# Feeding the first up block of a ConvFFN with the unnormalised residual

## The chip, the cores and the metric

The kernel runs on one core of a Trainium2 chip. Its time is the device time of one execution in microseconds; the number given for a kernel is the median of its runs. The engines are TensorE (PE in the profile, its weight loads PEld), VectorE (DVE), ScalarE (ACT), GpSimd (POOL) and SyncE (SP, which issues the loads of the weights). All of them run their own instructions in a fixed order and wait for each other by semaphores.

## The reference

The layer works on 256 latent tokens (with 256 context tokens beside them) of width 2048, in fp32. Only its second half matters here:

```
x = x + mod_x[2] * merge_branches(...)                     # gated residual; ends in @ w_out
x = x + mod_x[5] * conv_ffn(modulate(x, g_ffn, mod_x[3], mod_x[4]), w_up, conv_w, conv_b, w_down)

mod_x = split(silu(c) @ w_mod + b_mod, 6)                  # shift, scale, gate; twice
modulate(x, g, shift, scale) = rms_norm(x, g) * (1 + scale) + shift
conv_ffn(h): u = h @ w_up                                  # 2048 -> 2 x 5632
             u = depthwise conv of width 3 over the tokens, + conv_b
             a, g = split(u, 2);  return (silu(a) * g) @ w_down
```

The normalisation divides each token by the root of its mean square. So modulate(x) = r(token) * [x * g * (1 + scale)] + shift, and h @ w_up = r(token) * ([x * g * (1 + scale)] @ w_up) + shift @ w_up.

## The kernel before

Every product is fp32 taken apart into two fp32r halves, high and low, and summed from three products: high by high, low by high and high by low. Weights come from memory in pieces of 256 rows by 512 columns (512 KB, `wload`, issued by SP into seven buffers called raw). `wsplit` makes the halves of a piece: ScalarE copies the high part (L61, tile whi), VectorE subtracts to get the low part (L62, tile wlo), into three buffers each. One such piece for one projection is a tick: eight ticks make a block of 512 columns over all 2048 rows.

`tick` is where other work is put between the products. `defer(n, fn)` runs fn at the (n+1)th tick from now; matrix products and transposes issued there (`mm_b`, `turn_b`) are pinned behind the last product of the tick before. `bg_steps` is a list of small steps of which a tick takes `bg_rate` on average. The order on each engine is made by a planner that takes the ready instruction of highest priority by its own estimate of times; priority is program order, and the splitting of weights is raised above everything else.

The modulation vectors of the latent tokens are made by such steps (`mod_latent`): a step loads two raw pieces ahead, and VectorE multiplies the two 512-wide rows of one piece by a column of silu(c) and adds them up (L305 and L307, tile macc); after eight steps the sum is turned and reduced (L311, L313), and a deferred part sums it over partitions with a small product (tile pcl) and writes four columns. Three of the vectors (shift2, scale2, gcol1) are made during the mixing stages at a rate of 0.3, then 0.52, in the order 3, 4, 2; the fourth (gcol2, the last gate) at 0.36 in the up stage, 32 steps.

The output projection (`w_out`, four blocks, `proj_nat`) evacuates each bank by VectorE: times the gate (L920), added to the residual x1 (L921), and ScalarE sums the squares (L922). One and two ticks later TensorE turns the 128 x 512 result (`turn`, L81, tile ptx) and ScalarE copies it to x1T (L929). The gate as rows is made at the fifth tick of the first of these blocks (`rows_from_cols`, two small DMAs of GpSimd's queue).

Behind the four blocks the kernel finishes what is deferred (`flush`, L936), sums the squares (L938), makes the token factor (`rms_scale`, L353 to L359), spreads it over the partitions by a product with a diagonal (`token_rows`, L367 to L370, tile pr) and makes the input h2: for each of the 16 row tiles, VectorE scales (L417), ScalarE adds the shift and rounds to the high half (L418), VectorE makes the low half (L419). Then the up projection follows (`proj_pair`): 11 blocks, each of a side 0 (the half that goes through silu) and a side 1 (the other half). A tick here has 16 products of 128 x 512 or 256. `up_evac` adds the two halves of a bank (L973, L974), does the convolution (L975, L976, L978), and silu (L983) or the product of the sides (L985) and the split of the result. Six blocks make the first half and are followed by their part of the down projection; then come five blocks and the rest.

PSUM has eight banks: four of tag acc, one of tag main and three of tag side. In the up stage side 0 takes the four acc banks, side 1 takes main and the three side banks (tile accs). The deferred sums of gcol2 use main and are let in on side 0 only. The large SBUF tiles come from one pool of 16 (`M`).

Of the kernel before, what the change touches and what calls it, by code (L numbers as in the profile page):

```python
# [30 lines left out]
def layer_kernel(ctx, tc, A, out):  # L31
# [108 lines left out]

    beside = []
    later = []

    def defer(n, fn):

# [6 lines left out]
    def tick():  # L152

        pin[0] = last[0]
        for e in later:
            e[0] -= 1
        due = [e for e in later if e[0] < 0]
        later[:] = [e for e in later if e[0] >= 0]
        for e in due:
            e[1]()  # L160
        if beside:
            beside[2] += beside[1]
            while beside[2] >= 1.0:
                beside[2] -= 1.0
                next(beside[0], None)
        bg_rate[1] += bg_rate[0]
        while bg_rate[1] >= 1.0 and bg_steps:
            bg_rate[1] -= 1.0
            bg_steps.pop(0)()
        pin[0] = None  # L170
# [109 lines left out]

        return [lambda k0=k0: step(k0) for k0 in range(0, KT, nk)]

    def mod_latent(parts, put=lambda fn: defer(3, fn)):


        seq = [(part, dst, j, k0) for part, dst in parts for j in range(4) for k0 in range(0, KT, 2)]
        raws, a = {}, []

        def get(i):
            if i < len(seq) and i not in raws:  # L290
                part, _, j, k0 = seq[i]
                c0 = part * D + j * 512
                raws[i] = wload(w_mod[k0 * P:k0 * P + 256, c0:c0 + 512])

        def step(i):
            part, dst, j, k0 = seq[i]
            get(i)
            get(i + 1)
            if k0 == 0:
                a[:] = [W2("mod", "macc", [P, 512])]  # L300
            raw = raws[i]
            for k in range(2):
                kt = k0 + k
                if kt == 0:
                    V.tensor_scalar(a[0], raw[:, 0, :], ccol[:, 0:1], None, op0=ALU.mult)  # L305
                else:
                    V.scalar_tensor_tensor(a[0], raw[:, k, :], ccol[:, kt:kt + 1], a[0],  # L307
                                           op0=ALU.mult, op1=ALU.add)
            if k0 == KT - 2:
                tr = W2("mod", "mtr", [P, 16, 32])  # L310
                V.transpose(tr.rearrange("p a c -> p (a c)"), a[0])  # L311
                rs = sm.tile([P, 16], F32, name="mrs", tag="mrs", bufs=2)
                V.tensor_reduce(rs, tr, op=ALU.add, axis=AX.X)  # L313

                def out():
                    pc = bank("pcl", (32, 16))
                    mm_b(pc, sel[:, 0:32], rs, start=True, stop=True)
                    pv = pc.rearrange("p (a b) -> p b a", b=4)
                    d = dst[:, 4 * j:4 * j + 4]
                    for b4 in range(4):  # L320
                        V.tensor_copy(d[32 * b4:32 * b4 + 32, :], pv[:, b4, :])
                    b0 = part * 16 + j * 4
                    V.tensor_tensor(d, d, bmod[:, b0:b0 + 4], op=ALU.add)

                put(out)

        return [lambda i=i: step(i) for i in range(len(seq))]
# [16 lines left out]
    scale2 = cst.tile([P, KT], F32, name="scale2")  # L344
    gcol1 = cst.tile([P, KT], F32, name="gcol1")
    gcol2 = cst.tile([P, KT], F32, name="gcol2")

    def rms_scale(ss, n, shape):

# [321 lines left out]
        return vh, vl  # L671


    bg_steps.extend(mod_latent(((3, shift2), (4, scale2), (2, gcol1))))
    bg_rate[:] = [0.3, 0.0]

    qbt = M("qb", [P, 8, T])
# [203 lines left out]
    for j in range(4):  # L881
# [27 lines left out]
    x1 = [M(f"x1_{t}", [P, D]) for t in range(2)]  # L909
    for t in range(2):  # L910
        nc.sync.dma_start(x1[t], A["x"][0][t * P:(t + 1) * P, :])
    gate1 = []
    defer(4, lambda: gate1.append(rows_from_cols("gate1", gcol1)))
    x1T = [M(f"x1T{i}", [P, 8, T]) for i in range(2)]
    ss1 = sm.tile([P, 2, 4], F32, name="ss1", bufs=1)
    for j in range(4):
        def wo_evac(t, b, j=j):
            js = slice(j * 512, (j + 1) * 512)
# [5 lines left out]
            def turn():  # L924
                pt = bank("ptx1", (P, 4, P), side=True)
                for k in range(4):
                    turn_b(pt[:, k, :], x1[t][:, j * 512 + k * P:j * 512 + (k + 1) * P], ident)
                dst = x1T[j // 2][:, (j % 2) * 4:(j % 2) * 4 + 4, t * P:(t + 1) * P]
                S.activation(dst, pt, AF.Copy)  # L929
# [8 lines left out]
    V.tensor_reduce(s1, ss1, op=ALU.add, axis=AX.X)  # L938
# [20 lines left out]
    w_up, w_down = A["w_up"][0], A["w_down"][0]  # L959
    for half, blocks in enumerate((range(0, 6), range(6, 11))):  # L960
        n = len(blocks)
        ah = [M("ah", [P, 8, T], F32R) for _ in range((n + 1) // 2)]
        al = [M("al", [P, 8, T], F32R) for _ in range((n + 1) // 2)]
        for i, j in enumerate(blocks):
            u = [[W2("fc", "u", [P, 2, T]) for _ in range(2)] for _ in range(2)]

            def up_evac(f, b, side, j=j, u=u, i=i, ah=ah, al=al):
# [4 lines left out]
                us = W2("fa", "us", [P, T])  # L972
                S.activation(us, b[:, T:2 * T], AF.Copy)  # L973
                V.tensor_tensor(us, b[:, 0:T], us, op=ALU.add)  # L974
                S.activation(d, us, AF.Identity, scale=cw1[:, fi:fi + 1], bias=cb[:, fi:fi + 1])  # L975
                V.scalar_tensor_tensor(d[:, 1:T], us[:, 0:T - 1], cw0[:, fi:fi + 1], d[:, 1:T],  # L976
                                       op0=ALU.mult, op1=ALU.add)
# [9 lines left out]
                    split(ah[i // 2][:, q, :], al[i // 2][:, q, :], uu)  # L987

            for side in range(2):
                proj_pair(w_up, side * DFF + j * 512, ALL, lambda kt: h2[kt // 4][:, kt % 4, :, :],  # L990
                          up_banks(side), lambda f, b, side=side: up_evac(f, b, side))
        if half == 0:
            assert not bg_steps
            while sums:
                sums.pop(0)()
            flush()
            gate2 = rows_from_cols("gate2", gcol2)
        for j in range(4):
# [64 lines left out]
```

## Time and profile before

| what | value |
|---|---|
| median of 3 runs | 2040.28 us (2038.79 to 2041.38) |
| span of the profiled execution, first to last instruction | 2036.9 us |
| difference of the two | 3.4 us |
| TensorE busy | 1978.8 us, 97% |
| VectorE busy | 1429.5 us, 70% |
| ScalarE busy | 961.1 us, 47% |
| granted TensorE clock, mean | 0.993 |
| read from memory | 409.63 MB |

The page names its profiled execution by its span alone; the 3.4 us lie around it. Times in rows are counted from the start of the span. In a row of the timeline stand start, duration, engine, line, operation, result and inputs, count, and in brackets how long the engine had been idle and what released it. TensorE's matmuls overlap, so a group of four ends later than the sum of what each costs. A row of a view by stage gives the start and end, the length, and the busy time of each engine in that stretch.

### The profile page before, as it was taken

What the parts mean: (1) busy time and instruction counts of PE and PEld (TensorE: products, weight loads), DVE (VectorE), ACT (ScalarE), POOL (GpSimd) and SP (SyncE); (2) the same over time, 40 slices, a digit from 0 to 9 for tenths busy, and PEclk for the clock granted to TensorE, in tenths of its full rate; (3) what the DMA queues carried; (4) which work ended last, traced back from release to release, by engine and by line L of the source; (5) the groups of instructions that cost most, each with busy time, mean ns of one, the idle gap of its engine ahead of it and who ended that gap; (6) DMA issues with size and microseconds to landing.
All of it is one profiled execution on the core that took longest, in us unless ns stands there. A gap on an engine that the chain in (4) does not pass through costs nothing.

```text
span 2036.9 us, 27383 instructions
## 1 busy us (share of the span) xinstructions
PE 1978.8 (97%) x10384; PEld 1644.1 (81%) x10384; DVE 1429.5 (70%) x2237; ACT 961.1 (47%) x1394; POOL 42.5 (2%) x62
## 2 busy tenths in 40 slices
PE   6999999999999999999999999899999999999998
PEld 4678888887787777887787878688888888888887
DVE  4657577877748888877776455888887555667754
ACT  3323464553345556444344444565555434556532
POOL 0001000101000000000000000000000000000000
PEclk8999999999999999999999999899999999999999
DMA  9977223236544456788886655577775656555563
GB/s 351 355 259 232 86 83 93 87 121 207 182 137 133 125 171 217 249 281 275 273 276 227 236 199 188 193 249 247 265 254 196 212 193 194 187 187 187 194 211 111
DMA packets 214340, 413.54 MB, mean 203 GB/s; under 512 B 12548, under 2 KB 21092, under 8 KB 213184
## 3 DMA queue, kind: packets, MB, share of 16 engines
q1 hardware_dynamic: 212320, 406.89, 60.5%
q0 software_dynamic: 1360, 4.74, 0.8%
q8 instruction: 81, 1.33, 0.3%
q14 instruction: 51, 0.42, 0.1%
q10 hardware_dynamic: 528, 0.17, 0.0%
HBM read 409.63 MB, written 2.11 MB: 202 GB/s over the span
## 4 chain that ended last, share of the span: by engine, by line
PE 56%; DMA 8%; DVE 5%; issue 1%; ACT 0%; DVEq 0%; ACTq 0%
PE acc L68 40%; PE accs L68 12%; DMA raw<-in_w_mod 8%; DVE macc L307 2%; DVE wlo L62 1%; PE poa L78 1%; PE pS L78 1%; PE ptp L81 1%; PE pto L81 0%; ACT whi L61 0%; PE ptq L81 0%; DMA raw<-in_w_gla_o 0%; PE ptx L81 0%; DVE macc L305 0%; DVE s L811 0%
## 5 line engine op out<-in xcount | busy, mean ns | idle before, releaser
L61 ACT ACTIVATE whi<-raw 128x1024 fp32r<-128x1024 f32 x568 | 601.1, 1059 | 792.7 <-PE acc L68 623.5
L62 DVE TENSOR_TENSOR wlo<-raw,whi 128x1024 fp32r<-128x1024 f32 x568 | 693.0, 1224 | 324.5 <-ACT whi L61 303.4
L307 DVE SCALAR_TENSOR_TENSOR macc<-raw,ccol,macc 128x512 f32<-128x512 f32 x240 | 180.5, 752 | 116.1 <-DMA raw<-in_w_mod 112.3
L68 PE MATMUL acc<-h,whi 128*128 128x512 f32 x704 | 178.3, 395 | 2.2 <-DVE h L419 2.2
L68 PE MATMUL accs<-h,whi 128*128 128x512 f32 x704 | 176.3, 392 | 0.0
L68 PEld LDWEIGHTS acc<-h,whi 128*128 128x128 f32 x704 | 127.6, 190 | 25.6 <-DVE h L419 2.5
L68 PEld LDWEIGHTS accs<-h,whi 128*128 128x128 f32 x704 | 126.6, 189 | 22.6
L68 PE MATMUL acc<-whi,h00hi 128*128 128x512 f32 x352 | 140.5, 399 | 1.6 <-DVE kb L435 0.6
L68 PE MATMUL acc<-whi,h01hi 128*128 128x512 f32 x352 | 139.9, 398 | 0.0
L68 PE MATMUL acc<-whi,h00lo 128*128 128x512 f32 x352 | 138.3, 393 | 0.0
L68 PE MATMUL acc<-whi,h01lo 128*128 128x512 f32 x352 | 138.0, 392 | 0.0
L68 PE MATMUL acc<-whi,al 128*128 128x512 f32 x352 | 137.1, 389 | 0.0
L68 PE MATMUL acc<-whi,ah 128*128 128x512 f32 x352 | 137.0, 389 | 0.0
L68 PEld LDWEIGHTS acc<-h,wlo 128*128 128x128 f32 x704 | 96.2, 190 | 7.0
L68 PEld LDWEIGHTS accs<-h,wlo 128*128 128x128 f32 x704 | 96.0, 190 | 6.9
L68 PE MATMUL acc<-wlo,h01hi 128*128 128x512 f32 x352 | 97.1, 394 | 1.7 <-DVE wlo L62 1.7
L68 PE MATMUL acc<-h,wlo 128*128 128x256 f32 x704 | 98.3, 282 | 0.0
L68 PE MATMUL accs<-h,wlo 128*128 128x256 f32 x704 | 98.2, 282 | 0.0
L68 PE MATMUL acc<-wlo,h00hi 128*128 128x512 f32 x352 | 97.8, 393 | 0.0
L68 PE MATMUL acc<-wlo,ah 128*128 128x512 f32 x352 | 94.4, 389 | 0.0
L68 PEld LDWEIGHTS acc<-whi,h00hi 128*128 128x128 f32 x352 | 66.4, 189 | 15.7 <-DVE val L62 1.0
L68 PEld LDWEIGHTS acc<-wlo,h01hi 128*128 128x128 f32 x352 | 65.5, 188 | 15.8 <-DVE wlo L62 2.5
(373 smaller groups left out, 3463.6 us busy)
## 6 DMA issues: line engine op xcount, KB each, us to landing
raw<-in_w_in SPq DMA_DIRECT2D x208, 512.0 KB, 4.4
raw<-in_w_up SPq DMA_DIRECT2D x176, 512.0 KB, 3.5
raw<-in_w_mod SPq DMA_DIRECT2D x128, 512.0 KB, 4.2
raw<-in_w_down SPq DMA_DIRECT2D x88, 512.0 KB, 3.7
mraw<-in_w_mod SPq DMA_DIRECT2D x32, 1024.0 KB, 11.4
raw<-in_w_attn_o SPq DMA_DIRECT2D x32, 512.0 KB, 4.7
raw<-in_w_gla_o SPq DMA_DIRECT2D x32, 512.0 KB, 4.7
raw<-in_w_out SPq DMA_DIRECT2D x32, 512.0 KB, 3.6
```

The costliest lines, as they stand in the source:

```text
L61: S.activation(hi, src, AF.Copy)
L62: V.tensor_tensor(lo, src, hi.bitcast(F32), op=ALU.subtract)
L68: last[0] = PE.matmul(*a, **k).ins
L78: return after(PE.matmul(*a, **k))
L81: return after(PE.transpose(*a))
L307: V.scalar_tensor_tensor(a[0], raw[:, k, :], ccol[:, kt:kt + 1], a[0], op0=ALU.mult, op1=ALU.add)
```

## The change

- Side 0 of the first up block gets a new input, h2u = x1T * scale2 (with scale2 = (1 + scale) * g_ffn), split into halves, four row tiles after each block of the output projection. It has neither the token factor nor the shift.
- The result of that side, in `up_evac`, is multiplied by the token factor's row (rrow2) and gets a bias s2w = shift2 @ w_up[:, 0:512].
- s2w is made like the modulation vectors, by the same steps (now `matvec`, which takes any matrix and vector): 8 steps on the first 512 columns of w_up, at 0.4 per tick in the output projection. These columns are so read twice.
- There is no flush before the up stage. The last turns, the token factor (`second_norm`) and the normalised input h2 (`rows`, deferred once more) are made within the first up block; everything from its side 1 on uses h2.
- Every side of the up stage takes two acc banks; side 0 adds main and one side bank, side 1 two side banks. The deferred sums are let in on side 1, when they are at least four ticks old.
- The modulation vectors come in the order 2, 3, 4; the gate's rows are made in the last block before the output projection; gcol2's steps begin with block 1 instead of block 0 and run at 0.45 per tick.
- The tiles of the result (ah, al) are taken two blocks at a time, as they are needed.

```diff
-    def mod_latent(parts, put=lambda fn: defer(3, fn)):
+    def matvec(parts, put=lambda fn: defer(3, fn)):
-        seq = [(part, dst, j, k0) for part, dst in parts for j in range(4) for k0 in range(0, KT, 2)]
+        seq = [(part, j, k0) for part in parts for j in range(part[4]) for k0 in range(0, KT, 2)]
...
-    bg_steps.extend(mod_latent(((3, shift2), (4, scale2), (2, gcol1))))
+    def put_sum(fn):
+        if up_stage:
+            sums.append((count[0], fn))
+        else:
+            defer(3, fn)
+
+    up_stage = []
+    mods = [(w_mod, part * D, ccol, dst, 4, part * 16) for part, dst in
+            ((2, gcol1), (3, shift2), (4, scale2), (5, gcol2))]
+    bg_steps.extend(matvec(mods[:3], put_sum))
...
+        if j == 3:
+            gate1 = []
+            defer(3, lambda: gate1.append(rows_from_cols("gate1", gcol1)))
         proj_nat(A["w_gla_o"][0], 0, j * 512, ALL, [tok(gh, gl, 0), tok(gh, gl, 1)], mg_evac)
...
-    gate1 = []
-    defer(4, lambda: gate1.append(rows_from_cols("gate1", gcol1)))
...
+    defer(4, lambda: V.scalar_tensor_tensor(scale2, scale2, 1.0, gffn, op0=ALU.add, op1=ALU.mult))
+    bg_steps.extend(matvec([(w_up, 0, shift2, s2w, 1, None)], put_sum))
+    bg_rate[:] = [0.4, 0.0]
+    h2u, h2, rrow2 = [], [], []
...
                 S.activation(dst, pt, AF.Copy)
+                if t:
+                    h2u.append(M(f"h2u{j}", [P, 4, 2, T], F32R))
+                    for k in range(4):
+                        kt = 4 * j + k
+                        xk = x1T[kt // 8][:, kt % 8, :]
+                        hi, lo = h2u[j][:, k, 0, :], h2u[j][:, k, 1, :]
+                        S.activation(hi, xk, AF.Copy, scale=scale2[:, kt:kt + 1])
+                        V.scalar_tensor_tensor(lo, xk, scale2[:, kt:kt + 1], hi.bitcast(F32),
+                                               op0=ALU.mult, op1=ALU.subtract)
...
-    flush()
-    s1 = sm.tile([P, 2], F32, name="s1", bufs=1)
-    V.tensor_reduce(s1, ss1, op=ALU.add, axis=AX.X)
-    r1 = rms_scale(s1, D, [P, 2])
-    V.scalar_tensor_tensor(scale2, scale2, 1.0, gffn, op0=ALU.add, op1=ALU.mult)
-    rrow = token_rows("fb", "rrow", r1)
-    h2 = [M(f"h2{i}", [P, 4, 2, T], F32R) for i in range(4)]
-    for kt in range(KT):
-        xk = x1T[kt // 8][:, kt % 8, :]
-        affine_split(h2[kt // 4][:, kt % 4, 0, :], h2[kt // 4][:, kt % 4, 1, :], xk, rrow,
-                     scale2[:, kt:kt + 1], shift2[:, kt:kt + 1])
-    sums = []
-    bg_steps.extend(mod_latent([(5, gcol2)], sums.append))
-    bg_rate[:] = [0.36, 0.0]
+    def second_norm():
+        s1 = sm.tile([P, 2], F32, name="s1", bufs=1)
+        V.tensor_reduce(s1, ss1, op=ALU.add, axis=AX.X)
+        r1 = rms_scale(s1, D, [P, 2])
+
+        def rows():
+            pr = bank("pr", (P, T), side=True)
+            for t in range(2):
+                dg = sm.tile([P, P], F32, name="dg", tag="t128", bufs=2)
+                V.tensor_scalar(dg, ident, r1[:, t:t + 1], None, op0=ALU.mult)
+                mm_b(pr[:, t * P:(t + 1) * P], ones[:, 0:P], dg, start=True, stop=True)
+            rrow2.append(W2("fb", "rrow", [P, T]))
+            S.activation(rrow2[0], pr, AF.Copy)
+            h2.extend(M(f"h2{i}", [P, 4, 2, T], F32R) for i in range(4))
+            for kt in range(KT):
+                xk = x1T[kt // 8][:, kt % 8, :]
+                affine_split(h2[kt // 4][:, kt % 4, 0, :], h2[kt // 4][:, kt % 4, 1, :], xk, rrow2[0],
+                             scale2[:, kt:kt + 1], shift2[:, kt:kt + 1])
+
+        defer(0, rows)
+
+    defer(2, second_norm)
+    up_stage.append(1)
+    bg_rate[0] = 0.0
 
     def up_banks(side):
-        if side == 0:
-            while sums:
-                defer(3, sums.pop(0))
-            return [acc.tile([P, 512], F32, name="acc", tag="acc") for _ in range(4)]
-        return [bank("accs", side=(f > 0)) for f in range(4)]
+        if side:
+            while sums and count[0] - sums[0][0] >= 4:
+                defer(3, sums.pop(0)[1])
+        two = [acc.tile([P, 512], F32, name="acc", tag="acc") for _ in range(2)]
+        return two + [bank("accs", side=side or f) for f in range(2)]
...
+            if j == 1:
+                bg_steps.extend(matvec(mods[3:], put_sum))
+                bg_rate[:] = [0.45, 0.0]
...
+                if j == 0 and side == 0:
+                    V.tensor_tensor(us, us, rrow2[0], op=ALU.mult)
+                    S.activation(us, us, AF.Identity, bias=s2w[:, f:f + 1])
...
-                proj_pair(w_up, side * DFF + j * 512, ALL, lambda kt: h2[kt // 4][:, kt % 4, :, :],
+                hin = h2u if j == 0 and side == 0 else h2
+                proj_pair(w_up, side * DFF + j * 512, ALL, lambda kt, hin=hin: hin[kt // 4][:, kt % 4, :, :],
                           up_banks(side), lambda f, b, side=side: up_evac(f, b, side))
```

More of the change, by code (lines that the diff above doesn't have):

```diff
@@ L142, in layer_kernel @@
     later = []
+    count = [0]
     def defer(n, fn):
@@ L154, in tick @@
         pin[0] = last[0]
+        count[0] += 1
         for e in later:
@@ L290, in get @@
             if i < len(seq) and i not in raws:
-                part, _, j, k0 = seq[i]
-                c0 = part * D + j * 512
-                raws[i] = wload(w_mod[k0 * P:k0 * P + 256, c0:c0 + 512])
+                (w, c0, _, _, _, _), j, k0 = seq[i]
+                raws[i] = wload(w[k0 * P:k0 * P + 256, c0 + j * 512:c0 + (j + 1) * 512])
         def step(i):
-            part, dst, j, k0 = seq[i]
+            (_, _, vec, dst, _, b0), j, k0 = seq[i]
             get(i)
@@ L304, in step @@
                 if kt == 0:
-                    V.tensor_scalar(a[0], raw[:, 0, :], ccol[:, 0:1], None, op0=ALU.mult)
+                    V.tensor_scalar(a[0], raw[:, 0, :], vec[:, 0:1], None, op0=ALU.mult)
                 else:
-                    V.scalar_tensor_tensor(a[0], raw[:, k, :], ccol[:, kt:kt + 1], a[0],
+                    V.scalar_tensor_tensor(a[0], raw[:, k, :], vec[:, kt:kt + 1], a[0],
                                            op0=ALU.mult, op1=ALU.add)
@@ L321, in out @@
                         V.tensor_copy(d[32 * b4:32 * b4 + 32, :], pv[:, b4, :])
-                    b0 = part * 16 + j * 4
-                    V.tensor_tensor(d, d, bmod[:, b0:b0 + 4], op=ALU.add)
+                    if b0 is not None:
+                        V.tensor_tensor(d, d, bmod[:, b0 + j * 4:b0 + j * 4 + 4], op=ALU.add)
                 put(out)
@@ L346, in layer_kernel @@
     gcol2 = cst.tile([P, KT], F32, name="gcol2")
+    s2w = cst.tile([P, 4], F32, name="s2w")
     def rms_scale(ss, n, shape):
@@ L671, in v_block @@
         return vh, vl
-    bg_steps.extend(mod_latent(((3, shift2), (4, scale2), (2, gcol1))))
+    w_up, w_down = A["w_up"][0], A["w_down"][0]
+    sums = []
+    def put_sum(fn):
[7 more added lines that the diff above has]
+    bg_steps.extend(matvec(mods[:3], put_sum))
     bg_rate[:] = [0.3, 0.0]
@@ L947, in layer_kernel @@
-    sums = []
-    bg_steps.extend(mod_latent([(5, gcol2)], sums.append))
-    bg_rate[:] = [0.36, 0.0]
-    def up_banks(side):
-        if side == 0:
-            while sums:
-                defer(3, sums.pop(0))
-            return [acc.tile([P, 512], F32, name="acc", tag="acc") for _ in range(4)]
-        return [bank("accs", side=(f > 0)) for f in range(4)]
-    w_up, w_down = A["w_up"][0], A["w_down"][0]
+    def second_norm():
[16 more added lines that the diff above has]
+        defer(0, rows)
@@ L960, in layer_kernel @@
+    defer(2, second_norm)
+    up_stage.append(1)
+    bg_rate[0] = 0.0
+    def up_banks(side):
+        if side:
[3 more added lines that the diff above has]
+        return two + [bank("accs", side=side or f) for f in range(2)]
     for half, blocks in enumerate((range(0, 6), range(6, 11))):
         n = len(blocks)
-        ah = [M("ah", [P, 8, T], F32R) for _ in range((n + 1) // 2)]
@@ L963, in layer_kernel @@
-        al = [M("al", [P, 8, T], F32R) for _ in range((n + 1) // 2)]
+        ah, al = [], []
         for i, j in enumerate(blocks):
+            if i % 2 == 0:
+                ah.append(M("ah", [P, 8, T], F32R))
+                al.append(M("al", [P, 8, T], F32R))
+            if j == 1:
+                bg_steps.extend(matvec(mods[3:], put_sum))
+                bg_rate[:] = [0.45, 0.0]
             u = [[W2("fc", "u", [P, 2, T]) for _ in range(2)] for _ in range(2)]
@@ L994, in layer_kernel @@
             while sums:
-                sums.pop(0)()
+                sums.pop(0)[1]()
             flush()
```

## The prediction

> **What bounds the kernel now.** I read the page first, then the busy time by stage, then the chain of waits and the timeline at the one place where the stages show a hole.
>
> ```profile
> span 2036.9 us, 27383 instructions
> PE 1978.8 (97%) x10384; PEld 1644.1 (81%) x10384; DVE 1429.5 (70%) x2237; ACT 961.1 (47%) x1394; POOL 42.5 (2%) x62
> ```
>
> TensorE sets the time almost everywhere, so an edit pays only where TensorE stands still. The next view gives, for six stretches: length, then TensorE, weight loads, VectorE, ScalarE and GpSimd busy, then the granted clock, DMA share and GB/s.
>
> ```profile
> 839.00:1077.00 238.00, 234.26 (x1034) 188.41 (x1033) 177.78 (x230) 98.06 (x101) 0.00 (x0) 1.00 0.83 274
> 1191.50:1284.65 93.15, 91.45 (x418) 75.03 (x416) 53.71 (x57) 42.75 (x54) 1.07 (x2) 1.00 0.59 199
> 1284.65:1296.92 12.27, 2.45 (x12) 1.77 (x12) 8.31 (x21) 4.77 (x13) 0.00 (x0) 0.71 0.60 204
> 1296.92:1320.99 24.07, 24.07 (x129) 21.01 (x130) 22.21 (x39) 13.98 (x22) 0.00 (x0) 0.93 0.47 151
> 1320.99:1343.34 22.35, 22.35 (x129) 19.66 (x129) 18.10 (x27) 13.90 (x20) 0.00 (x0) 1.00 0.78 260
> 1343.34:1567.88 224.54, 224.54 (x1287) 197.23 (x1287) 189.85 (x289) 125.84 (x181) 0.00 (x0) 1.00 0.75 244
> ```
>
> Row two is the output projection, row three the hole behind it, rows four and five the first up block (one side each), row six the other five up blocks of the first half. In the hole TensorE works 2.45 us of 12.27, its clock falls to 0.71, and the block after it takes 24.07 us where the next one takes 22.35. The chain of waits and the timeline say what fills the hole:
>
> ```profile
> 1293.55 1.21 PE pr L368 x4
> ...
> 1296.92 24.07 PE acc L68 x128
> ```
> ```profile
> 1283.58 1.07 PE L68 MATMUL acc<-wlo,mh 128*128 128x512 f32 x4
> ...
> 1287.21 0.63 PE L81 MATMUL ptx<-ident,x 128*128 128x128 f32 x4 [2.57 <-DVE x L921]
> ...
> 1288.54 0.63 PE L81 MATMUL ptx<-ident,x 128*128 128x128 f32 x4 [0.70 <-DVE x L921]
> 1289.20 0.60 ACT L929 ACTIVATE x1T<-ptx 128x512 f32<-128x512 f32 x1
> 1290.00 1.54 DVE L307 SCALAR_TENSOR_TENSOR macc<-raw,ccol,macc 128x512 f32<-128x512 f32 x2 [1.61 <-DMA raw<-in_w_mod]
> 1291.46 0.15 DVE L938 TENSOR_REDUCE s<-ss 128x2 f32<-128x8 f32 x1
> ...
> 1293.11 0.48 DVE L367 TENSOR_SCALAR dg<-ident,rstd 128x128 f32<-128x128 f32 x2
> 1293.55 1.20 PE L368 MATMUL pr<-dg,ones 128*128 128x128 f32 x4 [4.38 <-DVE dg L367]
> ...
> 1296.92 3.57 PE L68 MATMUL acc<-h,whi 128*128 128x512 f32 x8 [2.18 <-DVE h L419]
> ```
>
> The last products of the output projection end at about 1284.65 (1283.58 + 1.07). The residual is updated and turned, the sum of squares becomes a token factor (with 1.61 us lost because a modulation step on VectorE waits for its load ahead of it), the factor is spread by a product, the first normalised piece is made, and only then does the first up product start.
>
> **The change, part by part.**
>
> *First up block on the unnormalised residual.* Its input h2u needs only x1T and scale2, so three quarters of it exist before the output projection ends; the last quarter is wanted at tick 7 of 8. A tick of this stage is 22.35 / 8 = 2.79 us, so that is 16.8 us in. The rows above have the second half turned 1288.54 + 0.63 - 1284.65 = 4.5 us after the end and copied at 5.2 us; in the new order the transposes stand behind ticks 1 and 2 (5.6 us), and four ScalarE and four VectorE passes follow: ready by about 9 us, 8 us early. So TensorE goes from one stage into the other with what is left of these three pieces of work inside the block: two groups of transposes and the spreading of the factor. A group costs TensorE this:
>
> ```profile
> 1260.84 1.07 PE L68 MATMUL acc<-wlo,mh 128*128 128x512 f32 x4
> ...
> 1263.56 1.07 PE L68 MATMUL acc<-wlo,mh 128*128 128x512 f32 x4
> ...
> 1266.76 1.08 PE L68 MATMUL acc<-wlo,mh 128*128 128x512 f32 x4
> ```
>
> The plain tick lasts 1263.56 - 1260.84 = 2.72 us, the next, with four transposes in it, 3.20: 0.48 each. The four instructions of the factor are of the same size; I take 0.48 for them too (between 0 and the 1.20 us that they take in the hole). The path from the end of the output projection to the second side was 12.27 + 24.07 = 36.34 us and becomes 22.35 + 3 x 0.48 = 23.79: **12.55 us saved**. It includes 1.72 us of slow clock (24.07 - 22.35). [...]
>
> *New waits on that path.* The transposes can stand in TensorE's queue before VectorE has updated the residual. At the first change of column block in the output projection it did happen:
>
> ```profile
> 1218.96 0.63 PE L81 MATMUL ptx<-ident,x 128*128 128x128 f32 x4 [1.70 <-issue]
> ```
>
> At the next two changes there was no such wait. Bounds: 0 to the 2.57 us of the hole; I take 0.6 (1.70 over three). It may also vanish at 1218.96, a gain of 1.7 at most. The factor's product stands behind tick 3, at 8.4 us; in the hole it was ready 1293.55 - 1284.65 = 8.9 us after the end, 1.61 of it the modulation step that no longer runs there, but now with three passes of weights before it on VectorE. Bounds 0 and the 4.38 us of its row; I take 0.7. Behind both stand all products of the block.
>
> *VectorE in the first block.* The durations come from starts, since neighbours overlap:
>
> ```profile
> 1297.58 1.27 DVE L417 SCALAR_TENSOR_TENSOR x1T<-x1T,scale,rrow 128x256 f32<-128x256 f32 x3
> 1298.76 0.88 DVE L419 SCALAR_TENSOR_TENSOR h<-x1T,shift,h 128x256 fp32r<-128x256 f32 x2
> ...
> 1301.62 1.23 DVE L62 TENSOR_TENSOR wlo<-raw,whi 128x1024 fp32r<-128x1024 f32 x1 [1.19 <-ACT whi L61]
> 1302.76 1.27 DVE L419 SCALAR_TENSOR_TENSOR h<-x1T,shift,h 128x256 fp32r<-128x256 f32 x3
> 1303.95 0.48 DVE L417 SCALAR_TENSOR_TENSOR x1T<-x1T,scale,rrow 128x256 f32<-128x256 f32 x1
> 1304.41 1.22 DVE L62 TENSOR_TENSOR wlo<-raw,whi 128x1024 fp32r<-128x1024 f32 x1
> ```
> ```profile
> L920 DVE TENSOR_TENSOR yo<-acc,gate x8: 684/686/692, 1216.4 to 1287.0; 128x512 f32<-128x512 f32 x8
> L974 DVE TENSOR_TENSOR us<-acc,us x44: 415/417/421, 1322.3 to 1903.2; 128x256 f32<-128x256 f32 x44
> ```
>
> A pass over 256 columns is 1.18 / 3 = 0.39 us, a low part of weights 1302.76 - 1301.62 = 1.14. Both sides of block 0 then hold 16 x 1.14 for weights, 4 x 0.69 for the last residual update, 4 x 0.39 for h2u, about 1.8 for the factor (1293.11 + 0.48 - 1291.46 = 2.1, gaps included), 32 x 0.39 = 12.5 for h2, and at most 8 x 0.39 + 8 x 0.42 = 6.5 for the first results (eight convolution passes, four additions and the four new multiplies): 43 us of 46. It fits, tightly; the stretch 1296.92 to 1320.99 already runs at 22.21 of 24.07 with no gap on TensorE. h2 is wanted by the second side, 22 us after the start; from about 10 us on VectorE has 1.65 us per tick for it, or two of its sixteen pieces, so some nine are there when the second side starts, which takes two per tick. ScalarE gets 16 passes for h2u and four for the bias, each at most the 0.60 us of the 512 columns at 1289.20, 12 us in all; at 42.75 of 93.15 and 13.98 of 24.07 it hides them. I book 0 here and price the failure as a rival.
>
> *The product of w_up's first columns with shift2.* Eight more loads of 512 KB and 16 more VectorE passes, in the first 20 ticks of the output projection. With the 12 passes of h2u that adds some 18 us to the 53.71 of 93.15 that VectorE works there, which the products hide. What can show is a load that is late on VectorE ahead of weights. The stage 839 to 1077 has such steps at 0.52 per tick and TensorE stands 238.00 - 234.26 = 3.74 us in it, 1.6%; at 0.4 per tick over 54 us I take 0.6, between 0 and 2. The longer order of modulation parts (gate first) moves nothing in number; the gate row goes to an earlier stage, and no row shows TensorE waiting for it now: 0 by that.
>
> *gcol2's steps.* Before, some ran already in the output projection; now all 32 begin with block 1 at 0.45 per tick. VectorE's row for the five blocks:
>
> ```profile
> L307 DVE SCALAR_TENSOR_TENSOR macc<-raw,ccol,macc 128x512 f32<-128x512 f32 x45 | 33.7, 750 | 16.3 <-DMA raw<-in_w_mod 15.7
> ```
>
> With the two first-row passes that the view lists apart these are 23.5 steps. A step of two passes with its share of the reduction occupies about 1.5 us, so 8.5 further steps bring 189.85 to 202.6 of 224.54, 90%; and 16.3 / 23.5 = 0.69 us of waiting for a load per step would bring it to 225, exactly full. A VectorE that comes later finds its load there, so much of that waiting goes; but bursts behind each block will show. Bounds: 0, as now, and 10 us (2.3 per block pair if every wait stays and the rate is kept within its 71 ticks). I take 2.0, nearer to the row of this stage, in which no TensorE gap is seen.
>
> *Banks alternating* is what lets the first block start while the last output banks are read; no other border between projections shows a wait, so 0 beyond that.
>
> Sum: 12.55 - 0.6 - 0.7 - 0.6 - 2.0 = **8.65 us** off. The profiled span is 2036.9; the runs' median of 2040.28 has 3.4 us around it, which stay. Span 2028.3, **time 2031.6 us**.
>
> **The rivals.**
>
> *Steps wait on VectorE, and it becomes the bound: slower.* The place is blocks 1 to 5. A product step that waits for its load holds every weight pass behind it. The stage 839 to 1077 shows what such steps wait at a high rate:
>
> ```profile
> L307 DVE SCALAR_TENSOR_TENSOR macc<-raw,ccol,macc 128x512 f32<-128x512 f32 x80 | 60.1, 752 | 57.0 <-DMA raw<-in_w_mod 55.4
> ```
>
> That is 55.4 / 40 = 1.39 us per step, twice the 0.69 of the up stage. If the 32 steps waited so in full: 202.6 + 44.5 = 247 against 224.5 of TensorE, 22.6 us lost, against 12.55 - 1.9 = 10.65 won: 2040.28 + 12 = 2052. It decides from about 1.0 us per step on. For it: VectorE at 90% and one queue. Against it: in 839 to 1077 VectorE worked 177.78 of 238.00, had time to wait, and cost TensorE only 1.6%. [...]
>
> *h2 in a lump: no change.* If its 32 passes stand ahead of the weights on VectorE, 12.5 us less the two prepared ticks of 2.79 leave a hole of 6.9, and 1.72 for the clock: 8.65 - 8.6, about 2040. Against it the interleaving at 1301.62 to 1304.41.
>
> *The change doesn't do what it says*: TensorE would stop at tick 7 for h2u's last quarter. At 8 us of margin, only if ScalarE or VectorE is blocked for that long; at 3 us of stop 2034.6, still faster.
>
> *Everything hides*: no new wait, and the one at 1218.96 gone: 12.55 + 1.7 = 14.3 off, 2026.0.
>
> **How the numbers follow.** Forecast 0.66 (mostly 2027.5 to 2036), all hidden 0.08, stop at tick 7 0.04, lump 0.12, VectorE the bound 0.10. A measurement of this kernel tells some 0.2%, 4.1 us, from no change. The forecast's range, the hidden case and the stop lie on the faster side: 0.78; the lump is mostly no change: 0.12; the bound slower: 0.10. The range reaches from the hidden case to the lump: 2026 to 2040.
>
> **What would show it.** Right: no TensorE gap over 2 us between the last output product and the first up product, the clock at 1.00 in the first up block, about 24 us for its first side and 22.4 for its second; the L307 passes of gcol2 waiting under 20 us in all. Wrong: TensorE waiting for a low part of weights in blocks 0 to 5; a wait for the factor's product above 2 us; L417 passes of h2 without weight passes among them; or blocks 1 to 5 longer than 224.5 us by more than 5.

## The result and the profile after

The changed kernel took 2024.70 us (median of 4 runs, 2021.45 to 2026.83), the kernel before 2039.53 us (median of 4) on the same chip: ratio 0.9921, 95% interval 0.9907 to 0.9935, so 13 to 19 us less. The forecast was 2031.6 us with a range of 2026 to 2040. The direction was right, the gain 14.8 us instead of the 8.65 forecast, and the time lies below the range.

The page of the changed kernel, first two lines:

```profile
span 2024.6 us, 27481 instructions
...
PE 1978.0 (98%) x10386; PEld 1645.4 (81%) x10386; DVE 1447.4 (71%) x2279; ACT 967.5 (48%) x1414; POOL 42.6 (2%) x62
```

TensorE is busy for as long as before (1978.8 us); what went is its idle time. The same view by stage as in the prediction, for the output projection, the two sides of the first up block, and the other five blocks:

```profile
1193.20:1284.82 91.62, 91.62 (x420) 75.45 (x420) 64.93 (x81) 46.98 (x65) 0.00 (x0) 1.00 0.70 244
1284.80:1308.80 24.00, 23.89 (x142) 20.87 (x141) 22.46 (x45) 16.78 (x31) 0.00 (x0) 1.00 0.54 177
1308.80:1331.20 22.40, 22.40 (x130) 19.72 (x129) 22.11 (x40) 17.95 (x30) 0.00 (x0) 1.00 0.65 209
1331.20:1555.80 224.60, 224.60 (x1288) 197.16 (x1287) 198.00 (x304) 125.58 (x183) 0.00 (x0) 1.00 0.78 260
```

The hole of 12.27 us is gone, the clock stays at 1.00, the first side takes 24.00 us (forecast: about 24), the second 22.40, the five blocks 224.60 against 224.54 before. The output projection, 93.15 us before, takes 91.62 and has no idle time left. The timeline at the border shows how the three leftover pieces lie between the products:

```profile
1283.75 1.07 PE L68 MATMUL acc<-wlo,mh 128*128 128x512 f32 x4
...
1284.65 1.07 PE L68 MATMUL acc<-h2u,whi 128*128 128x512 f32 x4
...
1287.42 0.60 PE L81 MATMUL ptx<-ident,x 128*128 128x128 f32 x4
...
1290.66 0.60 PE L81 MATMUL ptx<-ident,x 128*128 128x128 f32 x4
...
1292.66 1.66 DVE L957 SCALAR_TENSOR_TENSOR h2u<-x1T,scale,h2u 128x256 fp32r<-128x256 f32 x4
...
1294.44 0.48 DVE L973 TENSOR_SCALAR dg<-ident,rstd 128x128 f32<-128x128 f32 x2
...
1294.87 0.68 PE L78 MATMUL pr<-dg,ones 128*128 128x128 f32 x4
...
1295.59 0.38 ACT L976 ACTIVATE rrow<-pr 128x256 f32<-128x256 f32 x1 [1.00 <-PE pr L78]
...
1296.01 1.28 DVE L419 SCALAR_TENSOR_TENSOR x1T<-x1T,scale,rrow 128x256 f32<-128x256 f32 x3
...
1298.02 1.23 DVE L62 TENSOR_TENSOR wlo<-raw,whi 128x1024 fp32r<-128x1024 f32 x1
1298.43 1.07 PE L68 MATMUL accs<-h2u,whi 128*128 128x512 f32 x4
1299.17 1.27 DVE L421 SCALAR_TENSOR_TENSOR h<-x1T,shift,h 128x256 fp32r<-128x256 f32 x3
```

The first up product follows the last output product at once. Neither the transposes nor the factor's product has a bracket for idle time, and TensorE is busy for 23.89 of the 24.00 us: it stood for them by 0.11 us at most. The planner placed the factor's product 10 us into the block, within the fourth tick, where its input had just been made, and the passes that make h2 alternate with those for weights.

### The profile page after: what moved, and what is told of

It reads as the page before. It is cut to its first block, busy times and chain, and to the rows that moved or that the text cites. A ratio compares the mean times of both kernels' runs of the same rounds, so it can differ in the third digit from the quotient of the medians.

```text
span 2024.6 us, 27481 instructions
## 1 busy us (share of the span) xinstructions
PE 1978.0 (98%) x10386; PEld 1645.4 (81%) x10386; DVE 1447.4 (71%) x2279; ACT 967.5 (48%) x1414; POOL 42.6 (2%) x62
## 4 chain that ended last, share of the span: by engine, by line
PE 56%; DMA 8%; DVE 5%; issue 1%; ACT 1%; DVEq 0%; ACTq 0%
PE acc L68 41%; PE accs L68 12%; DMA raw<-in_w_mod 7%; DVE macc L308 2%; DVE wlo L62 2%; PE poa L78 1%; PE pS L78 1%; PE ptp L81 1%; ACT whi L61 0%; DMA raw<-in_w_gla_o 0%; PE pto L81 0%; PE ptx L81 0%; PE ptq L81 0%; DVE s L826 0%; DVE macc L306 0%
## 5 line engine op out<-in xcount | busy, mean ns | idle before, releaser
L68 PE MATMUL acc<-h,whi 128*128 128x512 f32 x672 | 183.8, 395 | 0.0
L68 PEld LDWEIGHTS acc<-h,whi 128*128 128x128 f32 x672 | 115.6, 190 | 15.1
L68 PEld LDWEIGHTS acc<-h,wlo 128*128 128x128 f32 x672 | 102.7, 189 | 13.1
L68 PE MATMUL accs<-h,wlo 128*128 128x256 f32 x672 | 108.0, 283 | 0.0
L68 PE MATMUL acc<-h,wlo 128*128 128x256 f32 x672 | 106.8, 282 | 0.0
L68 PEld LDWEIGHTS acc<-whi,h00hi 128*128 128x128 f32 x352 | 66.4, 189 | 14.9 <-DVE val L62 1.0
## 6 DMA issues: line engine op xcount, KB each, us to landing
mraw<-in_w_mod SPq DMA_DIRECT2D x32, 1024.0 KB, 10.2
```

What stands on the lines that cost most here:

```text
L68: last[0] = PE.matmul(*a, **k).ins
```

## The experiments

The table cuts each profiled execution at three events: the first product of the output projection, its last, and the first product of the down projection. In the kernels with the change the second and third pieces repeat within 0.3 us where the run alters nothing in them. In the four profiles with the old first block (before, e9, e5, e13) the third piece takes 282.1 to 283.7 us. The first piece takes 1188.9 to 1195.1 us in all kernels but e8 and e12, which alter the steps in it. The ratios are to the kernel before on the same chip.

| kernel | ahead of output proj. | output proj. | to first down product | rest | median, us (runs) | ratio, 95% interval |
|---|---|---|---|---|---|---|
| before | 1191.5 | 93.2 | 283.0 | 469.2 | 2039.53 (4) | 1 |
| changed | 1193.2 | 91.6 | 271.0 | 468.8 | 2024.70 (4) | 0.9921 [0.9907, 0.9935] |
| e9, before again | 1193.3 | 93.3 | 282.7 | 469.2 | 2041.36 (12) | 1.0001 [0.9990, 1.0012] |
| e1, changed again | 1188.9 | 91.6 | 271.0 | 468.7 | 2022.51 (5) | 0.9914 [0.9900, 0.9927] |
| e2, h2 for the first block | 1192.4 | 91.6 | 282.4 | 468.8 | 2035.97 (11) | 0.9979 [0.9970, 0.9988] |
| e3, gate late | 1191.2 | 98.4 | 271.0 | 468.7 | 2030.73 (5) | 0.9952 [0.9939, 0.9964] |
| e5, before + gate early | 1195.1 | 91.1 | 283.7 | 469.2 | 2037.65 (12) | 0.9985 [0.9975, 0.9996] |
| e13, before + order 2, 3, 4 | 1189.5 | 91.5 | 282.1 | 469.2 | 2041.89 (12) | 1.0001 [0.9991, 1.0011] |
| e11, order 3, 4, 2 | 1190.9 | 91.6 | 271.0 | 468.7 | 2024.06 (5) | 0.9915 [0.9902, 0.9929] |
| e7, no s2w | 1191.1 | 91.2 | 271.0 | 468.8 | 2023.19 (6) | 0.9917 [0.9901, 0.9932] |
| e6, h2 raised | 1190.1 | 91.6 | 271.0 | 468.7 | 2023.21 (6) | 0.9910 [0.9896, 0.9923] |
| e4, gcol2 at 0.9 | 1189.7 | 91.6 | 298.7 | 468.4 | 2048.12 (5) | 1.0043 [1.0028, 1.0058] |
| e8, earlier steps at 0.40 | 1207.9 | 94.3 | 271.0 | 468.8 | 2044.10 (12) | 1.0017 [1.0008, 1.0025] |
| e12, earlier steps at 0.60 | 1203.8 | 91.6 | 271.2 | 468.7 | 2037.75 (11) | 0.9983 [0.9974, 0.9992] |

### Both kernels again (e1, e9)

Both kernels once more, unaltered.

> The changed kernel once more, unaltered, to see which stage carries the spread between its executions (2021.45 to 2026.83 us) and whether the 2.5 us by which the medians differ beyond the two profiled spans belongs to the change. Theory A (the gain is the hole plus the late gate, about 13.6 us in the stages that the change touches; the rest is spread of the start): output projection 91.6 us and output projection's end to the down projection 271.0 us again, both within 0.3; the stretch before the output projection differs from 1193.2 by up to 5 us; median within 3 us of 2024.7. Theory B (the change gives more than 13.6 us, in some executions): these two stages come out shorter than 91.6 and 271.0 together by 2 us or more.

> The kernel before, once more, for its stages. Theory A (the change is worth its two stages, 1.5 and 12.1 us; the rest of the difference of the medians is spread of the stretch ahead of the output projection): output projection 93.2 us and from its end to the down projection 283.0 us again, within 0.3; the stretch ahead of it between 1188.9 and 1193.2, as in the five profiles with the change. Theory B (the new order of the modulation parts makes the stretch ahead of it shorter too, by 2 to 3 us): 1193.5 or more here.

Measured: the two pieces repeat to 0.3 us in both kernels. They give 1.6 us (93.2 to 91.6) and 11.9 us (282.85, the mean of two, to 271.0), and 0.5 behind them: 14.0 us. The medians give more, 14.8 and 17.4. The first piece was 1193.3 in this second profile of before; the expectation would have called 1193.5 or more a gain of the change there, so this alone decides nothing.

### The main part undone (e2)

```diff
-    defer(2, second_norm)
+    flush()
+    second_norm()
+    flush()
...
-                if j == 0 and side == 0:
-                    V.tensor_tensor(us, us, rrow2[0], op=ALU.mult)
-                    S.activation(us, us, AF.Identity, bias=s2w[:, f:f + 1])
...
-                hin = h2u if j == 0 and side == 0 else h2
+                hin = h2
```

> The main part undone: the first up block takes the normalised input again, which is made behind a flush before the up stage, without the token factor and the bias on its result; h2u and shift2 @ w_up are still made and not used. Everything else of the change stays (gate early, banks alternating, gcol2 from block 1 at 0.45). Theory A (hole of 36.4 us becomes 24.0): TensorE gap of 9 to 10 us, clock near 0.7 in it, the first side about 24 us; 12 us above the repeat, about 2037; the output projection stays at 91.6. Theory C (the new waits of 1.3 us and the fuller VectorE that I booked exist and are paid out of the gain): only about 9 us above the repeat, 2034.

Measured: 13.5 us above the repeat by the medians of the same chip, 11.4 by the piece. The view by stage and the timeline of TensorE show the old hole:

```profile
1284.00:1296.30 12.30, 3.22 (x14) 2.44 (x15) 8.88 (x24) 6.29 (x17) 0.00 (x0) 0.67 0.26 83
1296.30:1320.40 24.10, 24.10 (x133) 21.01 (x132) 19.56 (x34) 14.81 (x25) 0.00 (x0) 0.96 0.49 141
```
```profile
1286.18 0.63 PE L81 MATMUL ptx<-ident,x 128*128 128x128 f32 x4 [2.20 <-DVE x L941]
1287.51 0.63 PE L81 MATMUL ptx<-ident,x 128*128 128x128 f32 x4 [0.70 <-DVE x L941]
1292.15 1.20 PE L78 MATMUL pr<-dg,ones 128*128 128x128 f32 x4 [4.02 <-DVE dg L973]
1295.53 2.07 PE L68 MATMUL acc<-h,whi 128*128 128x512 f32 x4 [2.18 <-DVE h L421]
```

Length 12.30 us, clock 0.67, first side 24.10: close to the 12.27, 0.71 and 24.07 of before, with all other parts of the change in place. From the border to the second side that is 36.40 us against 24.00 in the changed kernel, 12.40 more; the other five blocks came out 1.0 us shorter here (223.60), which is why the piece shows 11.4. So the hole and its slow clock are what the first block's input is worth, nearly all of the 12.55 us worked out; theory C, that the booked waits were paid out of it, falls.

### The gate's rows (e3, e5, e13, e11)

e3 is the changed kernel with the gate back in the output projection:

```diff
-        if j == 3:
-            gate1 = []
-            defer(3, lambda: gate1.append(rows_from_cols("gate1", gcol1)))
...
+    gate1 = []
+    defer(4, lambda: gate1.append(rows_from_cols("gate1", gcol1)))
```

e5 is the kernel before with the opposite edit, and the parts in the order 2, 3, 4, which it needs. e13 has that order alone, e11 is the changed kernel with the order 3, 4, 2.

> The changed kernel with the gate's rows made in the fifth tick of the output projection again, as before the change. Theory A (the wait of 1.70 us ahead of the first transposes was the gate's DMA, which lands 7.5 us after its issue): the first L940 pass starts about 2 us after its products end, TensorE stands 1.5 to 1.7 us at the first transposes, output projection 93.1 us; 1.5 us above the repeat. Rival (the wait came from the planner's order of VectorE and is gone with the new order): no wait, output projection 91.6, 0 us.

> The kernel before with one part of the change: modulation parts in the order 2, 3, 4 and the gate's rows made in the last block ahead of the output projection. Theory A (the wait of 1.70 us was the late gate): no wait at the first transposes, output projection 91.6 us, the rest as before: 1.5 us off, 2038. Rival (it needs the other parts too, since the late gate alone with all other parts cost 6.8 us): output projection still 93 us.

> The kernel before with one thing altered: the modulation parts in the order 2, 3, 4. Nothing but the columns of w_mod that are loaded when is different ahead of the output projection. Theory B' (the 2 us by which the kernels with parts of the change are faster than their stages say come from that order): 2 us off, ratio about 0.999, output projection 93.2. Theory A: ratio 1.000 within 0.001; what the 2 us come from then stays open.

> The changed kernel with the modulation parts in the order 3, 4, 2 as before the change, the gate's rows still early. On every engine the instructions ahead of the output projection then differ from those of the changed kernel by nothing but the columns of w_mod that are loaded when. Theory A (what is left of the difference of the medians beyond the two stages, 2 to 3 us, has nothing to do with that order): the stretch ahead of the output projection between 1188.9 and 1193.2 and the median within 2 us of the repeats' 2022.5 to 2024.7. Theory B (the order is worth 2 to 3 us): 2025 to 2027.

The timeline of before, read again at the end of the first column block of the output projection:

```profile
1208.98 0.55 POOL L338 DMA_DIRECT2D gate<-dgate  x1 [3.90 <-PE acc L68]
...
1213.47 1.07 PE L68 MATMUL acc<-wlo,mh 128*128 128x512 f32 x4
...
1216.43 0.69 DVE L920 TENSOR_TENSOR yo<-acc,gate 128x512 f32<-128x512 f32 x1 [3.16 <-PE acc L68]
```

The block's products end at 1214.5, but the first multiplication by the gate starts at 1216.43, 7.45 us after the gate's DMA was issued. The row puts the idle time down to TensorE's bank, which had been done for 1.9 us. The view of DMA issues, whose last figure is the time from issue to landing, has this for the stretch around it:

```profile
gate<-dgate POOLq DMA_DIRECT2D x1, 1024.0 KB, 7.4
```

The gate landed at 1216.4, just when VectorE starts. The second profile of the same kernel (e9) names it:

```profile
1210.76 0.55 POOL L338 DMA_DIRECT2D gate<-dgate  x1 [3.89 <-PE acc L68]
...
1218.37 0.69 DVE L920 TENSOR_TENSOR yo<-acc,gate 128x512 f32<-128x512 f32 x1 [3.31 <-DMA gate<-dgate]
```

With the order of the parts alone altered and the gate still late (e13) the DMA landed 5.8 us after its issue, and the profiled execution lost nothing at the transposes; the output projection took 91.5. This execution was the fastest of its twelve, 2034.11 us where their median is 2041.89:

```profile
1206.88 0.55 POOL L338 DMA_DIRECT2D gate<-dgate  x1 [3.87 <-PE acc L68]
...
1212.80 0.69 DVE L920 TENSOR_TENSOR yo<-acc,gate 128x512 f32<-128x512 f32 x1 [1.60 <-DMA gate<-dgate]
```

In the changed kernel the same DMA is issued 32 us before its use, and VectorE starts when the products allow:

```profile
1183.47 0.55 POOL L339 DMA_DIRECT2D gate<-dgate  x1 [2.58 <-PE acc L68]
...
1215.74 0.69 DVE L940 TENSOR_TENSOR yo<-acc,gate 128x512 f32<-128x512 f32 x1 [0.85 <-PE acc L68]
```

So theory A holds for the wait of 1.70 us, with an addition: what the late gate costs is not fixed, since the landing varies (7.4 us in before, 7.5 in e9, 5.8 in e13, which issues it from the same place); what makes it vary was not tested. By the medians of e5 an early gate is worth 3.1 us (ratio 0.9985, interval 0.4 to 2.5 thousandths, 0.8 to 5.1 us); its profiled execution shows 2.1 in the output projection. Order alone gives no difference that the runs can tell: 1.0001 for e13, with an interval of some 2 us to either side, and e11 lies within the repeats.

e3 cost 6.8 us in the output projection where 1.5 was expected, and 8.2 by the medians (2030.73 against 2022.51). VectorE and TensorE at the same place, the landing of its gate, and the stretch around it:

```profile
1209.69 0.55 POOL L339 DMA_DIRECT2D gate<-dgate  x1 [4.89 <-PE acc L68]
...
1215.86 1.07 PE L68 MATMUL acc<-wlo,mh 128*128 128x512 f32 x4
...
1218.17 1.54 DVE L308 SCALAR_TENSOR_TENSOR macc<-raw,shift,macc 128x512 f32<-128x512 f32 x2 [4.36 <-DMA raw<-in_w_up]
1219.62 0.68 DVE L939 TENSOR_TENSOR yo<-acc,gate 128x512 f32<-128x512 f32 x1
...
1222.14 1.09 PE L81 MATMUL ptx<-ident,x 128*128 128x128 f32 x4 [5.21 <-issue]
```
```profile
gate<-dgate POOLq DMA_DIRECT2D x1, 1024.0 KB, 5.3
```
```profile
1217.00:1240.00 23.00, 17.86 (x77) 14.88 (x78) 16.30 (x21) 9.70 (x16) 0.00 (x0) 0.93 0.65 223
```

The gate itself was not late in this execution. Issued at 1209.69, it landed at 1215.0, ahead of the end of the block's products at 1216.9 (1215.86 + 1.07). But on VectorE one of the new product steps (two passes) stands ahead of the gate's multiplication, and VectorE waited 4.36 us for its load. That the planner chose this order because it counted on a late gate is likely, since nothing but the place of the gate's rows differs, but it was not shown. TensorE then stood 5.21 us at the transposes, and its clock fell: 0.93 over 23 us is 1.6 us more, and 5.2 + 1.6 = 6.8. So e3 prices this order, not the landing; theory A rests on before, e9 and e5. The place of the gate and the new steps act together: 2.1 us for the gate in e5, 0.4 for the steps in e7, 6.8 here.

### The new steps on VectorE (e7, e4, e8, e12)

e7 leaves the product out (`V.memset(s2w, 0.0)` in place of the steps); e4 sets gcol2's rate (the first pair of lines), e8 that of the earlier modulation steps (the second pair; e12 sets 0.6 there):

```diff
-                bg_rate[:] = [0.45, 0.0]
+                bg_rate[:] = [0.9, 0.0]
...
-    bg_rate[0] = 0.52
+    bg_rate[0] = 0.4
```

> The changed kernel without the eight steps that make shift2 @ w_up for the first columns: s2w is zero, so this part of the computation is left out. Theory A (the 4 MB of loads and the 12 us on VectorE lie wholly behind the products): output projection 91.6 us and the up stage 271.0 us as before, 0 us. The prediction's term of 0.6 us for late loads: output projection 91.0 us.

> The gcol2 steps at 0.9 per tick instead of 0.45, so 32 steps in 36 ticks instead of 71. Theory A (VectorE's load waits shrink when it is behind, and the prepared weight pieces cover the rest): blocks 1 and 2 of the up stage fill VectorE to about 1.14 + 0.9 x 1.5 + 0.75 = 3.2 us per tick against 2.79, so TensorE must stand about 0.4 us per tick, 12 to 15 us in all; 2038. Theory D (the planner spreads the steps by its own order, whatever the rate): no change, 2024.7 within 1.5. Slower rival of the prediction (each step waits in full for its load): 32 x 1.39 = 44 us on top of a full VectorE, 2055 or more.

> The changed kernel with the earlier modulation steps spread thinner, at 0.40 per tick instead of 0.52, over the stages between attention and the output projection; the work is the same. TensorE stands 4.7 us there for low parts of weights in the profile of the changed kernel. If the rate of the steps sets these waits: 2 us or less of waits, the stretch from the first attention output product to the output projection 339 us or shorter, and 2 to 3 us off the changed kernel. If they come from single late loads: no change.

> The changed kernel with the earlier modulation steps at 0.60 per tick instead of 0.52; at 0.40 VectorE waited 119 us for their loads instead of 57 and the stretch from the first attention output product to the output projection took 358.1 us instead of 341.6. If fewer ticks between the steps let VectorE find its loads there: waits under 57 us, stretch 339 or shorter, 2 to 3 us off. If the shared load buffers run out, as at 0.9 in the up stage: ScalarE waits for weights, stretch 345 or longer.

e7: 91.2 against 91.6 us, and 2023.19 against 2022.51 to 2024.70: the eight steps cost 0.4 us by the stage, and the medians can't tell that from nothing. It is not a late load, since TensorE has no idle time in this stretch with the steps either (91.62 us busy of 91.62). In the changed kernel VectorE's row for gcol2's steps over the six up blocks is this:

```profile
L308 DVE SCALAR_TENSOR_TENSOR macc<-raw,ccol,macc 128x512 f32<-128x512 f32 x60 | 44.9, 749 | 14.9 <-DMA raw<-in_w_mod 14.2
```

Counted as in the prediction, without the first-row passes that are listed apart (1.3 us more), the 32 steps wait 14.9 us, 0.47 each instead of 0.69. VectorE, at 198.00 of 224.60 us in blocks 1 to 5, never holds TensorE, which is busy for all 224.60: the term of 2.0 us was 0. At 0.9 per tick (e4) the piece grows by 27.7 us, twice what was expected, and not by the road I had in mind. Its waits in the up stage, who waited for whom, in us, times and longest:

```profile
ACT whi L61 <- DMA raw<-in_w_up: 46.5, 21, 4.9
```
```profile
PE acc L68 <- ACT whi L61: 15.7, 12, 3.4
```

No step waits on VectorE for its load any more; ScalarE waits for weights, and TensorE 15.7 us for ScalarE. Of the 27.7 us, 19 are idle time of TensorE and 8.6 longer busy time (279.5 us in this piece against 270.9), with a granted clock of 0.97 and 0.92 in the two stretches of 45 us from 1327 on. The steps' loads take the same seven buffers, and the weights come late. The view does not tell buffers from the order of issue on SP, so which of the two makes them late is not settled.

The earlier steps, between attention and the output projection, were to yield 2 to 3 us by a better rate. Both directions lost. VectorE and TensorE in that stretch, first the waits of VectorE in the changed kernel, then e8 with its row of busy times, then e12:

```profile
DVE macc L308 <- DMA raw<-in_w_mod: 53.9, 34, 3.2
DVE wlo L62 <- ACT whi L61: 46.5, 33, 2.1
```
```profile
DVE macc L308 <- DMA raw<-in_w_mod: 114.9, 39, 4.9
```
```profile
849.80:1207.90 358.10, 341.70 (x1487) 272.89 (x1486) 233.41 (x287) 142.59 (x148) 1.07 (x2) 1.00 0.73 243
```
```profile
PE acc L68 <- DVE wlo L62: 16.1, 18, 1.8
```
```profile
DVE macc L308 <- DMA raw<-in_w_mod: 46.4, 28, 4.4
```
```profile
PE acc L68 <- DVE wlo L62: 10.2, 13, 2.5
```

At 0.40 the steps wait twice as long as at 0.52, and the stretch from the first attention output product on takes 358.1 us instead of 341.6; at 0.60 they wait less and it takes 351.8. Neither of e8's two theories, a gain or no change, came true. In e8 VectorE works 233.4 us and waits 123.9 us for the loads of steps (114.9 in the line above, 9.0 for first-row passes), together 357.3 of 358.1, and its passes for weights never wait for ScalarE. So VectorE has become the bound there: this is the prediction's slower rival at work in another stage. TensorE's waits for low parts of weights explain 11.4 of the 16.5 us lost (16.1 against 4.7 in the changed kernel); the rest is longer busy time (341.7 against 336.6), whose cause is open.

In e12 the stretch is longer than the 345 us that were expected if the load buffers ran out, but ScalarE waits for no late weights there, so that cause is not the one. TensorE waits 5.5 us more than in the changed kernel; why the higher rate loses as well was not found. One possibility is that the planner's estimate, more than the rate, decides where a step stands against its load.

### h2 in a lump (e6)

```diff
-            for kt in range(KT):
-                xk = ...
+            with tc.high_priority():
+                for kt in range(KT):
+                    xk = ...
```

> The changed kernel with the 48 instructions that make h2 raised to the priority of the weights, so that they come in one piece ahead of the weights that the planner has not placed yet. The prediction's rival 'h2 in a lump': 12.5 us on VectorE less two prepared ticks gives a hole of about 6.9 us and 1.7 of slow clock, 8.6 us above the changed kernel, 2031. Other theory (ScalarE's part of each piece leaves VectorE gaps that the planner fills with weights, or the prepared pieces last longer): under 2 us.

Measured: 271.0 us, as without it, which is the other theory's number. The raised priority did not make a lump: VectorE's timeline has the passes of weights among those of h2 at the same places as in the changed kernel. The likely reason, not tested further, is that the weights are raised too and are ready each time before ScalarE has finished its part of the next piece. So the rival's price was not tested; the run stands as a third one of the changed kernel's program order.

## Why the prediction was right or wrong

**The hole: right.** It was worked out as 36.34 us becoming 23.79. It became 24.00, and undoing this part alone brought back 12.30 us at clock 0.67. The transposes and the factor's product were put at 1.44 us in the block; the side's excess over a plain one is 24.00 - 22.40 = 1.6. The last quarter of h2u was ready at 1294.3 (1292.66 + 1.66), 9.5 us after the border where about 9 was worked out, so the stop at tick 7 did not come.

**The new waits: wrong, 1.3 us that did not come.** The transposes found the residual updated: it was ready at 1288.2 (1287.50 + 0.69) and 1286.9, they ran at 1290.66 and 1287.42. The factor's product was taken to stand right behind tick 3, at 8.4 us, and to wait there. Tick 3 is only the earliest place for it, and it ran 10.2 us into the block, where its input had just been made.

**The product with shift2: wrong, 0.6 us that did not come.** I took 0.6 us for late loads from the idle share of another stage, 1.6%. TensorE waits for nothing in the output projection; the 0.4 us between e7 and the changed kernel are busy time, which the sum had at nothing.

**gcol2's steps: wrong, 2.0 us that did not come, the largest term in error.** The work was sized about right: 202.6 us forecast for VectorE, 198.00 measured. The waits shrank from the 22 us of the bound to 14.9, as the reason given for it (a VectorE that comes later finds its load there) would have it, but what was left of them cost TensorE nothing either; no burst behind a block shows. The row of the stage itself, no gap at 85% of VectorE, was the better guide than a value between the bounds.

**The gate: the step that failed most in kind.** "No row shows TensorE waiting for it now: 0 by that." The row was on my desk: the wait of 1.70 us at 1218.96, which I put down to transposes standing in TensorE's queue ahead of VectorE's update. I booked 0.6 us for more of it in the new block, and named its going away only as a chance, without a cause. The gate's DMA at 1208.98 and its landing 7.4 us later lead to 1216.4, where VectorE starts. The output projection shows 1.5 us for it in the profiled executions; by the medians of e5 it is 3.1, with an interval of 0.8 to 5.1.

**The sum.** 8.65 forecast, plus 3.9 for the three terms that were 0 or nearly, plus 1.5 for the gate, is 14.05; the pieces measured 14.0. That the two agree so closely is in part luck: the hole's piece gave 11.9 us instead of 12.55, and 0.5 came behind it, in a part where the sum had nothing; the cause of that is open. The case "everything hides", 14.3 us, was the one that came, and it had been given 0.08.

**The frame of the sum** was off as well. I set the span of 2036.9 us against the median of the runs and read 3.4 us around it. The profiled executions give 1.8 (2026.38 against 2024.6, and 2040.29 against 2038.5 for e9), so the profiled execution of before was one of its faster ones. Such a difference carries the spread of the runs with it. The lower end of the range did so too: 2026.0 is the hidden case taken off one median, 2040.28, with nothing for the spread of the runs. Off the 2039.53 measured beside the change the same 14.3 us give 2025.2, and 2024.70 came.

**What stays open.** The medians differ by 14.8 to 17.6 us in the five runs of the changed program or near it, the pieces by 14.0. If a late gate costs 3.1 us in the median instead of the 1.6 of the profiles, that accounts for 1.5 of it, and e2 and e5 together give 13.5 + 3.1 = 16.6; but the interval of e5 holds 1.6 as well. That the rest is spread of the first piece is likely from its 1188.9 to 1195.1 us, but with one profile per run it was not shown.

**The rivals.** The slower one did not decide at 0.45 per tick. Doubling the rate made the kernel slower than before by 8.2 us in the medians (ratio 1.0043), through late weights rather than through steps waiting on VectorE; the road that it named was seen in e8. A step that holds a weight pass can be seen in before as well: VectorE stood 1.91 us until 852.12 for the load of one, with the high half of the pass behind it done at 851.39 (850.33 + 1.06). The price of h2 in a lump was not tested, since e6 made none.

## What to carry to other kernels

Where one engine sets the time, a hole in it can be priced from the rows around it, here to within about half a microsecond: its length (12.27 us), plus the slow clock behind it (1.72 us), less what of its work must still run between the products. When the work that used to fill the hole is moved behind products, look at whether its engine left any gap on the bounding engine at a similar load before booking new waits. And when a row blames an engine that had long been done, look for a DMA issued some microseconds earlier: its issue time plus the time to its landing tells (here 1208.98 + 7.4 us), and a second profile may name it outright.

## What the runs showed of the hardware

- TensorE's clock after a stop: 1.70 us of idleness (before, at 1218.96) left it at 1.00; 5.21 us (e3) brought it to 0.93 over the 23 us that begin with the stop, 1.6 us more; and behind the 12.3 us of the hole, with little work in it, the first side took 1.72 us longer than the second in before (24.07 against 22.35, clock 0.93) and 1.70 in e2 (24.10 against 22.40, clock 0.96). The price was not the same each time, though: in e5 the first side behind a hole of 12.1 us took 25.22 us at clock 0.88, 2.9 more than the plain 22.35.
- A DMA that spreads one row of 8 KB over all partitions landed 7.4 and 7.5 us after its issue in two executions of the kernel before, 5.8 and 5.3 in e13 and e3, all issued in the first block of the output projection, and 11.3 us after it in the changed kernel and in e1, which issue it ahead of that stage.
- Behind the first piece the kernels with the change repeat to 0.3 us wherever TensorE does not stop; the four profiles with the hole differ by 1.6 us in its piece, some 1.4 of which is the longer first side of e5 (25.22 against 23.83 us in e13). The first piece differs by up to 6 us; what sets it was not found.
